# A hybrid decoder layer on one core: six and four feed-forward column tiles by plain products ahead of the seven-product units, in place of four and two

## The chip, the cores and the metric

The kernel runs on one core of a Trainium2 chip. The metric is the device time of one execution in microseconds (us); lower is better. The profile of one further execution is read beside it.

## What is computed

One decoder layer on 512 tokens of width 1024, all in float32. Two SwiGLU feed-forwards with an inner width of 2816 stand around a token mixer (sliding-window attention and a gated causal convolution), and a gated embedding ends the layer. The two feed-forwards are what the change touches:

```python
def swiglu(h, w_gu, w_down):
    g, u = jnp.split(h @ w_gu, 2, axis=-1)
    return (jax.nn.silu(g) * u) @ w_down

def reference(x, p, ffn1_norm, ffn1_wgu, ffn1_wdown, mix_norm, w_in, ...):
    x = x + 0.5 * swiglu(rmsnorm(x, ffn1_norm[i]), ffn1_wgu[i], ffn1_wdown[i])
    ...
    x = x + merged @ w_out[i]
    x = x + 0.5 * swiglu(rmsnorm(x, ffn2_norm[i]), ffn2_wgu[i], ffn2_wdown[i])
    e = rmsnorm(p[i] @ ple_proj[i], ple_norm[i])
    gate = jax.nn.sigmoid(rmsnorm(x, ple_gate_norm[i]) @ ple_gate_w[i])
    x = x + gate * e
```

## The kernel before

Each float32 product is made of three fast ones. Every operand is split into a rounded high part and the remainder (`split_into`: ScalarE writes the high part, VectorE subtracts it to get the low part), and `mm3` adds high times high, low times high and high times low in PSUM. So a weight piece of 128x1024 costs one ScalarE and one VectorE instruction (`whi_wgu`, `wlo_wgu`) before TensorE may use it.

**Two ways to make a feed-forward's gate and up columns.** The 2816 columns are 22 tiles of 128, each with a gate half and an up half.

- A tile by *plain products* (`products`, called from `ffn`): 2 halves x 8 blocks of the width x 3 products = 48 matmuls with 512 tokens moving. It uses the activations before normalization (tiles `h` in the first feed-forward, `f_h` in the second) and multiplies by the norm's factor only when the sums leave PSUM (`gated`: VectorE writes `f_gs` and `f_us`, ScalarE does the SiLU, GpSimd multiplies by the factor). It therefore needs no factor before it starts. Each tile holds two PSUM banks (`f_g`, `f_u`) until `gated` has read them.
- Two tiles by a *unit* (`pair` and `unit`): Strassen's scheme, seven products in place of eight, on halves of the tokens. That is 7 forms x 2 halves x 4 blocks x 3 = 168 matmuls with 256 tokens moving, summed in the banks `wgu_a` and `wgu_b`. It needs sums of weight blocks (two made by accumulating DMAs from GpSimd's queue, two by VectorE in the PSUM tiles `zs_wgu`) and forms of the *normalized* activations: `f_xn` (x times gain times factor), its split `f_nh`, `f_nl`, and the sums and differences `f_t` with their splits `f_t_h`, `f_t_l`. `sums` makes these once for each feed-forward, mostly on VectorE, and they cannot start before the norm's factor is in the PSUM tile `f_n_sp`.

**The order in `ffn`.** Tiles 0 and 1 go by plain products block by block while the norm is computed. Then `plain - 2` further tiles go by plain products, `sums` is recorded, the plain tiles are gated, and the rest goes by units, two tiles at a time. The first down projection of the first four pairs (`down(0, 4)`, tiles `wd`) follows the unit that starts at tile 8, the others the last unit:

```python
PLAIN = 4, 2
DOWNS = {8: [(0, 4)], 20: [(4, 8), (8, 11)]}
```

`PLAIN` gives the number of plain tiles in the first and the second feed-forward; so before there are 9 + 10 = 19 units.

**What sets the order on the engines.** Nothing is run as it is recorded. `record` makes a list of virtual instructions, `plan` and `simulate` order them for each engine by due times worked back from TensorE's order, with numbered slots for buffers (4 for raw weights, 4 each for high and low parts, 8 PSUM banks), and `hybrid_layer` issues them. On the chip each engine then works through its own list in that order. `SUMMED` names the weights of the mixer whose remainder is made by an accumulating DMA (`residue`) and not by VectorE.

Of the kernel before, what the change touches and what calls it, by code (L numbers as in the profile page):

```python
# [20 lines left out]
KD = D // P  # L21
# [379 lines left out]
        op.ls = ls  # L401


SUMMED = dict(wzc=1, wzg=1)
WINDOW = 10
PLAIN = 4, 2
DOWNS = {8: [(0, 4)], 20: [(4, 8), (8, 11)]}
SPARE = 0, 1, 3, 6

# [273 lines left out]
def record():  # L683
    nc = Program()

    def ps_tile(name):
        return nc.tile(name, [P, S], F32, "ps")
# [24 lines left out]
    def split_into(hi, lo, src, scale=None, eng=nc.vector):  # L712
        if scale is None:
            nc.scalar.activation(hi, src, AF.Copy)
            eng.tensor_tensor(lo, src, hi.bitcast(F32), op=ALU.subtract)
        else:
            nc.scalar.activation(hi, src, AF.Copy, scale=scale)
            nc.vector.scalar_tensor_tensor(
                lo, src, scale, hi.bitcast(F32), op0=ALU.mult, op1=ALU.subtract
            )  # L720
# [5 lines left out]

    def piece(key, i, n=PIECE, off=0, cuts=1):

        if key in SUMMED and i % SUMMED[key] == 0:
            return residue(key, i)  # L730
        raw = nc.tile(f"raw_{key}{i}", [P, PIECE], F32, "raw")
        hi = nc.tile(f"whi_{key}{i}", [P, PIECE], F32R, "hi")
        lo = nc.tile(f"wlo_{key}{i}", [P, PIECE], F32R, "lo")
        for c in range(cuts):
            s = slice(c * n // cuts, (c + 1) * n // cuts)
            d = slice(off + s.start, off + s.stop)
            nc.sync.dma_start(raw[:, s], Dram(key)[i][:, d])
            split_into(hi[:, s], lo[:, s], raw[:, s], eng=nc.flex if key in FLEX else nc.vector)
        return hi, lo

    def residue(key, i):

        raw = nc.tile(f"raw_{key}{i}", [P, PIECE], F32, "raw")
        hi = nc.tile(f"whi_{key}{i}", [P, PIECE], F32R, "hi")
        rest = nc.tile(f"wlo_{key}{i}", [P, PIECE], F32R, "lo")
        nc.sync.dma_start(raw, Dram(key)[i])
        nc.scalar.activation(rest, raw, AF.Copy, scale=-1.0)
        nc.scalar.activation(hi, raw, AF.Copy)
        nc.gpsimd.dma_start(rest, raw, accum_op=ALU.add)
        return hi, rest  # L750

    def mm3(ps, w, x, start, stop, first=1, skip=False):

        nc.tensor.matmul(ps, w[first], x[0], start=start, stop=False, skip_group_check=skip)
        nc.tensor.matmul(ps, w[1 - first], x[0], start=False, stop=False, skip_group_check=skip)
        nc.tensor.matmul(ps, w[0], x[1], start=False, stop=stop, skip_group_check=skip)

    def part(w, s):
        return w[0][:, s], w[1][:, s]
# [270 lines left out]
    def ffn(tag, wgu, wdown, h, gain, ss, after, cuts, wide, plain, mid=None):  # L1030
# [9 lines left out]
        def products(i, ks):  # L1040
            if i not in gu:
                gu[i] = ps_tile(f"{tag}_g{i}"), ps_tile(f"{tag}_u{i}")
            for k in ks:
                if k % 4 == 0:
                    ws[i] = piece(wgu, 2 * i + k // 4, cuts=cuts)
                if k == ks[0]:
                    cm = nc.group(f"{tag}_gu{i}_{k}")
                    cm.__enter__()
                c = (k % 4) * 256
                for j, ps in enumerate(gu[i]):  # L1050
                    mm3(
                        ps, part(ws[i], slice(c + j * P, c + (j + 1) * P)), h[k], k == 0, k == KD - 1,
                        0 if cuts > 1 and i == k == 0 else 1,
                    )
            cm.__exit__(None, None, None)
# [93 lines left out]
                first = first or nc.groups[-1].ops[0]  # L1149
        for i in range(plain):  # L1150
            if i > 1:
                products(i, range(4))
                products(i, range(4, KD))
        T, hn = sums(tag, gain, rp)
        for i in range(plain):
            for ps in gu[i]:
# [9 lines left out]
    def next_norm(tag, gain):  # L1166
        h, ss = [None] * KD, SumSq(f"{tag}_ss")

        def after(o):
            h[o] = split(f"{tag}_h{o}", x[o], gain[:, o : o + 1])  # L1170
            ss.in_psum(x[o], KD)

        return h, ss, after

    h2, ss2, after = next_norm("mix", g_mix)
    ffn("f1", "wgu1", "wd1", h, g_ffn1, ss, after, 4, False, PLAIN[0])


    def proj(tag, key, i, h, nk=KD):

        w = piece(key, i)
        ps = ps_tile(tag)
        with nc.group(tag):
            for k in range(nk):
                mm3(ps, part(w, slice(k * P, (k + 1) * P)), h[k], k == 0, k == nk - 1)
        return ps
# [65 lines left out]
    def token_major(tag, key, i0, n_pieces, kper, n):  # L1252

        per = S // n
        banks = [ps_tile(f"{tag}b{b}") for b in range(NT // per)]
        pss = [banks[t % len(banks)][:, (t // len(banks)) * n :][:, 0:n] for t in range(NT)]
        ws = [piece(key, i0 + i) for i in range(n_pieces)]
        with nc.group(tag):
            for t0 in range(0, NT, len(banks)):
                for i in range(n_pieces):  # L1260
                    for kk in range(kper):
                        k = i * kper + kk
                        wk = part(ws[i], slice(kk * n, (kk + 1) * n))
                        for t in range(t0, t0 + len(banks)):
                            xk = part(h2[k], slice(t * P, (t + 1) * P))
                            mm3(pss[t], xk, wk, k == 0, k == KD - 1)
        return pss
# [216 lines left out]
    def embedding(i):  # L1484

        if not pin:
            for k in range(KP):
                t = ftile(f"pin{k}")
                nc.sync.dma_start(t, Dram("pT")[k])
                pin.append(split(f"pin{k}", t))  # L1490
        w = piece("wple", i)
        for j in range(4):
            n = 4 * i + j
            ps = ps_tile(f"e{n}")
            with nc.group(f"e{n}"):
                for k in range(KP):
                    c = (j * KP + k) * P
                    mm3(ps, part(w, slice(c, c + P)), pin[k], k == 0, k == KP - 1)
            e = ftile(f"es{n}")
            nc.scalar.copy(e, ps)  # L1500
            es.append(e)
            sse.add(ps, on_act=True)
        if len(es) == KD:
            rbe = spread("ple", mean_rstd("ple", sse.accs, D))
            for o in range(KD):
                nc.vector.scalar_tensor_tensor(
                    es[o], es[o], g_ple[:, o : o + 1], rbe, op0=ALU.mult, op1=ALU.mult
                )
# [31 lines left out]

    h4, ss4, after4 = next_norm("pg", g_gate)
    ffn("f2", "wgu2", "wd2", h3, g_ffn2, ss3, after4, 1, False, PLAIN[1], lambda: [embedding(i) for i in range(2)])


# [173 lines left out]
```

## Time and profile before

| | |
|---|---|
| median of three runs | 1165.48 us (1165.45 to 1166.0) |
| the profiled execution | 1165.91 us, of which the profile's span is 1164.2 us |
| TensorE matmuls | 7628 records, busy 98% of the span |
| VectorE | busy 84% of the span |
| ScalarE, GpSimd | 62% and 34% |
| granted TensorE clock, mean | 0.995 |

Times within the profile are us from the start of the span. A row of a timeline has the start, the length and the instruction, with output and inputs by the program's names. A row of windows has, for a stretch, the busy time of TensorE (PE), its weight loads (PEld), VectorE (DVE), ScalarE (ACT) and GpSimd (POOL), each with its number of instructions, then the granted TensorE clock (1.00 is full), the busy share of the DMA engines and GB/s. The first feed-forward lies at 5 to 354 us, the mixer up to about 758, the second feed-forward at 758 to about 1110, and the gate of the embedding at the end. Matmuls overlap, so that the time of one is read from the distance between starts and not from its length.

### The profile page before, as it was taken

Reading aid. Unit: us, or ns where it says so; the run is one execution under the profiler, and the core shown is the slowest. Engines: PE = TensorE matmul, PEld = TensorE weight load, DVE = VectorE, ACT = ScalarE, POOL = GpSimd, SP = SyncE. Lnnn points to the kernel's source line nnn. Section 1 sums busy time; section 2 is a strip of 40 time slices with the busy share of each in tenths; the row PEclk is TensorE's granted clock in tenths of the full one; section 3 lists DMA queues with packets and bytes.
Section 4 is the critical chain, followed back from the end, with each engine's and each line's share of the span. In section 5 each row is a group of like instructions: output and inputs, shape, how many; then the busy total and the mean of one; then the engine's idle time right before and its main releaser. Section 6 shows DMA issues by size and latency. Waiting matters only on the chain.

```text
span 1164.2 us, 20217 instructions
## 1 busy us (share of the span) xinstructions
PE 1145.0 (98%) x7628; PEld 1052.0 (90%) x7628; DVE 977.2 (84%) x1660; ACT 722.3 (62%) x1279; POOL 395.0 (34%) x480
## 2 busy tenths in 40 slices
PE   9999999999999999999999999999999999999998
PEld 7889999999998888878888888888999999999976
DVE  7899978889896799988998865589888788679996
ACT  6556446656366699999984753355663566574541
POOL 1523113321113886885687100033221132242000
PEclk9989999999999999999999999999999999999999
DMA  7556666566547472665654532435666665565521
GB/s 242 137 146 163 157 159 152 164 144 177 128 123 190 115 176 64 155 145 127 146 162 121 133 109 91 113 87 137 169 158 162 145 174 127 146 153 142 139 73 73
DMA packets 51363, 163.69 MB, mean 141 GB/s; under 512 B 6208, under 2 KB 10944, under 8 KB 51264
## 3 DMA queue, kind: packets, MB, share of 16 engines
q1 hardware_dynamic: 37584, 114.12, 30.1%
q0 software_dynamic: 13536, 48.24, 24.3%
q8 instruction: 60, 0.98, 0.3%
q14 instruction: 39, 0.32, 0.1%
q10 hardware_dynamic: 144, 0.03, 0.0%
HBM read 143.50 MB, written 2.10 MB: 125 GB/s over the span
## 4 chain that ended last, share of the span: by engine, by line
PE 88%; DVE 7%; ACT 4%; DMA 1%; issue 1%; POOL 0%; DVEq 0%; POOLq 0%; ACTq 0%
PE wgu_b L1605 17%; PE wgu_a L1605 12%; PE wd_b L1605 11%; PE wd_a L1605 8%; PE gb L1605 4%; PE ap L1605 4%; PE cp L1605 4%; PE wo L1605 4%; PE pg L1605 3%; PE cb L1605 3%; PE ga L1605 3%; PE ca L1605 3%; PE q0b L1605 2%; PE q1b L1605 2%; DVE wlo_wgu L1605 2%; PE f_g L1605 2%
## 5 line engine op out<-in xcount | busy, mean ns | idle before, releaser
L1605 DVE TENSOR_TENSOR wlo_wgu<-raw_wgu,whi_wgu 128x1024 fp32r<-128x1024 f32 (+1 forms) x131 | 137.1, 1055 | 38.5 <-ACT whi_wgu L1605 38.5
L1605 ACT ACTIVATE whi_wgu<-raw_wgu 128x1024 fp32r<-128x1024 f32 (+1 forms) x131 | 116.2, 901 | 75.1 <-PE wgu_b L1605 33.3
L1605 PE MATMUL wgu_b<-f_t_h,wlo_wgu 128*128 128x256 f32 x456 | 130.2, 285 | 4.5 <-DVE f_gs L1605 2.2
L1605 PE MATMUL wgu_b<-f_t_l,whi_wgu 128*128 128x256 f32 x456 | 130.0, 285 | 2.2 <-DVE f_t_l L1605 2.2
L1605 POOL DMA_DIRECT2D raw_wgu<-in_wgu x38 | 33.6, 900 | 284.4 <-DVE x L1605 123.2
L1605 PE MATMUL wgu_b<-f_t_h,whi_wgu 128*128 128x256 f32 x456 | 129.5, 284 | 0.0
L1605 ACT ACTIVATE whi_wd<-raw_wd 128x1024 fp32r<-128x1024 f32 (+1 forms) x60 | 59.3, 989 | 94.6 <-PE wd_b L1605 58.5
L1605 POOL TENSOR_TENSOR y<-y,ct 128x511 f32<-128x511 f32 (+27 forms) x90 | 108.2, 1242 | 10.4 <-DVE wlo_wap L1605 3.7
L1605 DVE SCALAR_TENSOR_TENSOR cz<-u,dww,cz 128x510 f32<-128x510 f32 (+28 forms) x145 | 106.6, 735 | 3.3
L1605 PEld LDWEIGHTS wgu_b<-f_t_h,wlo_wgu 128*128 128x128 f32 x456 | 88.0, 193 | 5.4 <-DVE f_gs L1605 1.6
L1605 PEld LDWEIGHTS wgu_b<-f_t_l,whi_wgu 128*128 128x128 f32 x456 | 88.0, 193 | 3.0 <-DVE f_t_l L1605 3.0
L1605 PEld LDWEIGHTS wgu_b<-f_t_h,whi_wgu 128*128 128x128 f32 x456 | 88.1, 193 | 0.0
L1605 PE MATMUL wgu_a<-f_nh,wlo_wgu 128*128 128x256 f32 x304 | 86.1, 283 | 0.0
L1605 PE MATMUL wgu_a<-f_nh,whi_wgu 128*128 128x256 f32 x304 | 86.0, 283 | 0.0
L1605 PE MATMUL wgu_a<-f_nl,whi_wgu 128*128 128x256 f32 x304 | 86.0, 283 | 0.0
L1605 DVE TENSOR_TENSOR wlo_wd<-raw_wd,whi_wd 128x1024 fp32r<-128x1024 f32 (+1 forms) x60 | 69.1, 1151 | 10.0 <-ACT whi_wd L1605 9.6
L1605 PE MATMUL wd_a<-f_f_h,wlo_wd 128*128 128x256 f32 x264 | 74.7, 283 | 0.0
L1605 PE MATMUL wd_a<-f_f_h,whi_wd 128*128 128x256 f32 x264 | 74.7, 283 | 0.0
L1605 PE MATMUL wd_a<-f_f_l,whi_wd 128*128 128x256 f32 x264 | 74.7, 283 | 0.0
L1605 PE MATMUL wd_b<-f_f_h,wlo_wd 128*128 128x256 f32 x264 | 74.7, 283 | 0.0
L1605 PE MATMUL wd_b<-f_f_h,whi_wd 128*128 128x256 f32 x264 | 74.7, 283 | 0.0
L1605 PE MATMUL wd_b<-f_f_l,whi_wd 128*128 128x256 f32 x264 | 74.7, 283 | 0.0
(505 smaller groups left out, 4019.5 us busy)
## 6 DMA issues: line engine op xcount, KB each, us to landing
raw_wgu<-in_wgu SPq DMA_DIRECT2D x80, 512.0 KB, 4.4
raw_wgu<-in_wgu POOLq DMA_DIRECT2D x38, 512.0 KB, 5.5
raw_wd<-in_wd SPq DMA_DIRECT2D x32, 512.0 KB, 4.5
raw_wd<-in_wd POOLq DMA_DIRECT2D x16, 512.0 KB, 5.5
raw_wzc<-in_wzc SPq DMA_DIRECT2D x16, 512.0 KB, 3.7
wlo_wzc<-raw_wzc POOLq DMA_DIRECT2D x16, 512.0 KB, 5.3
raw_wzg<-in_wzg SPq DMA_DIRECT2D x16, 512.0 KB, 4.0
wlo_wzg<-raw_wzg POOLq DMA_DIRECT2D x16, 512.0 KB, 5.2
```

Source lines behind the costliest of these rows:

```text
L1605: made[op] = getattr(engines[op.eng], op.what)(*a, **k)
```

## The change

```diff
-SUMMED = dict(wzc=1, wzg=1)
+SUMMED = dict(wzc=0, wzg=0)
 WINDOW = 10
-PLAIN = 4, 2
+CUT = 4
+PLAIN = 6, 4
...
-        if key in SUMMED and i % SUMMED[key] == 0:
+        if key in SUMMED and i >= SUMMED[key]:
             return residue(key, i)
...
         for i in range(plain):
             if i > 1:
-                products(i, range(4))
-                products(i, range(4, KD))
+                for k in range(0, KD, CUT):
+                    products(i, range(k, k + CUT))
```

The numbers of plain tiles go from 4 and 2 to 6 and 4, so that each feed-forward has one unit less. The condition on `SUMMED` is true for every piece of the two weights in both forms, and with `KD = 8` and `CUT = 4` the loop over `k` gives the same two calls as before.

The engines' lists show it as follows. TensorE's list in the first feed-forward, at the end of the fourth plain tile (`f_u_550`): before, the first unit (`wgu_b`) follows at once.

```order
L1605 MATMUL f_u_550<-h_7_h,wlo_wgu_454 128x512
L1605 MATMUL f_u_550<-h_7_h,whi_wgu_412 128x512
L1605 MATMUL f_u_550<-h_7_l,whi_wgu_412 128x512
L1605 MATMUL wgu_b_648<-f_nh_490,wlo_wgu_1_585 128x256
L1605 MATMUL wgu_b_648<-f_nh_490,whi_wgu_1_473 128x256
L1605 MATMUL wgu_b_648<-f_nl_600,whi_wgu_1_473 128x256
```

In the changed kernel the same place (`f_u_562` is the fourth tile's) goes on to the fifth plain tile, `f_g_673`:

```order
L1606 MATMUL f_u_562<-h_7_h,wlo_wgu_461 128x512
L1606 MATMUL f_u_562<-h_7_h,whi_wgu_414 128x512
L1606 MATMUL f_u_562<-h_7_l,whi_wgu_414 128x512
L1606 MATMUL f_g_673<-h_0_h,wlo_wgu_600 128x512
L1606 MATMUL f_g_673<-h_0_h,whi_wgu_477 128x512
L1606 MATMUL f_g_673<-h_0_l,whi_wgu_477 128x512
```

The first unit comes behind the sixth tile, 96 matmuls later:

```order
L1606 MATMUL f_u_787<-h_7_h,wlo_wgu_705 128x512
L1606 MATMUL f_u_787<-h_7_h,whi_wgu_685 128x512
L1606 MATMUL f_u_787<-h_7_l,whi_wgu_685 128x512
L1606 MATMUL wgu_b_873<-f_nh_504,wlo_wgu_1_744 128x256
L1606 MATMUL wgu_b_873<-f_nh_504,whi_wgu_1_733 128x256
L1606 MATMUL wgu_b_873<-f_nl_756,whi_wgu_1_733 128x256
```

So 96 plain matmuls have moved in ahead of the first unit, and one unit of 168 is gone further on; the second feed-forward does the same. TensorE's list has 7433 rows before and 7289 now, 144 = 2 x (168 - 96) fewer. From the end of the first down projection to the start of the second feed-forward the lists of all engines read as before, but for one ScalarE instruction (the split of the embedding's input, `pin_h`) that stands 18 places later; from the second feed-forward's first down projection on they read as before again.

VectorE's list in the first feed-forward, where it makes the activation forms of the first unit. Before: `zs_wgu` sums weights in PSUM, `f_gs_692` gates the last plain tile, `wlo_wgu_6` and `wlo_wgu_5` are the weights of forms 6 and 5, `f_gs_718` and `f_us_735` belong to the unit's own results.

```order
L1605 SCALAR_TENSOR_TENSOR f_t_0_702<-f_t_0_487,f_xn_529 128x256
L1605 SCALAR_TENSOR_TENSOR f_t_1_715<-f_t_1_505,f_xn_546 128x256
L1605 TENSOR_TENSOR wlo_wgu_6_723<-zs_wgu_0_675,whi_wgu_6_694 128x512
L1605 TENSOR_TENSOR f_gs_718<-wgu_b_648,f_gs_718 128x256
L1605 SCALAR_TENSOR_TENSOR f_t_1_715<-f_t_1_505,f_xn_566 128x256
L1605 TENSOR_TENSOR f_t_0_l<-f_t_0_702,f_t_0_h 128x512
L1605 TENSOR_TENSOR wlo_wgu_6_723<-zs_wgu_1_682,whi_wgu_6_694 128x512
L1605 TENSOR_TENSOR wlo_wgu_5_743<-raw_wgu_21_416,whi_wgu_5_612 128x1024
L1605 TENSOR_TENSOR f_t_1_l<-f_t_1_715,f_t_1_h 128x512
L1605 SCALAR_TENSOR_TENSOR f_us_757<-f_u_550,f_gs_692 128x512
L1605 TENSOR_TENSOR f_t_0_l<-f_t_0_487,f_t_0_h 128x512
L1605 TENSOR_TENSOR f_t_1_l<-f_t_1_505,f_t_1_h 128x512
```

In the changed kernel, `f_gs_875` gates the sixth plain tile, whose bank is `f_g_779`:

```order
L1606 TENSOR_TENSOR wlo_wgu_5_854<-raw_wgu_21_647,whi_wgu_5_828 128x1024
L1606 TENSOR_TENSOR f_t_0_l<-f_t_0_838,f_t_0_h 128x512
L1606 TENSOR_TENSOR f_t_1_l<-f_t_1_845,f_t_1_h 128x512
L1606 TENSOR_TENSOR f_gs_875<-f_g_779,f_n_rb 128x512
L1606 TENSOR_TENSOR f_t_0_l<-f_t_0_494,f_t_0_h 128x512
L1606 TENSOR_TENSOR wlo_wgu_6_892<-zs_wgu_0_820,whi_wgu_6_879 128x512
L1606 TENSOR_TENSOR wlo_wgu_6_892<-zs_wgu_1_830,whi_wgu_6_879 128x512
L1606 TENSOR_TENSOR f_t_1_l<-f_t_1_551,f_t_1_h 128x512
L1606 TENSOR_TENSOR f_gs_917<-wgu_b_873,f_gs_917 128x256
L1606 SCALAR_TENSOR_TENSOR f_us_928<-f_u_787,f_gs_875 128x512
```

The splits of the activation forms (`f_t_0_l`, `f_t_1_l`) and of the weights 5 and 6 stand ahead of the first result of the unit (`f_gs_917`), where before they stood behind it (`f_gs_718`).

VectorE's list in the second feed-forward, from the gating of its plain tiles on. Before (`f_g_8629` and `f_g_8642` are the two plain tiles):

```order
L1605 TENSOR_TENSOR f_gs_8865<-f_g_8629,f_n_rb 128x512
L1605 SCALAR_TENSOR_TENSOR f_t_0_8872<-f_t_0_8737,f_xn_8761 128x256
L1605 SCALAR_TENSOR_TENSOR f_t_0_8872<-f_t_0_8737,f_xn_8772 128x256
L1605 TENSOR_TENSOR f_gs_8883<-f_g_8642,f_n_rb 128x512
L1605 TENSOR_TENSOR wlo_wgu_6_8893<-zs_wgu_0_8662,whi_wgu_6_8848 128x512
L1605 SCALAR_TENSOR_TENSOR f_t_1_8901<-f_t_1_8756,f_xn_8781 128x256
L1605 TENSOR_TENSOR wlo_wgu_6_8893<-zs_wgu_1_8669,whi_wgu_6_8848 128x512
L1605 SCALAR_TENSOR_TENSOR f_t_1_8901<-f_t_1_8756,f_xn_8789 128x256
L1605 TENSOR_TENSOR f_t_0_l<-f_t_0_8872,f_t_0_h 128x512
L1605 TENSOR_TENSOR f_gs_8907<-wgu_b_8859,f_gs_8907 128x256
L1605 SCALAR_TENSOR_TENSOR f_us_8941<-f_u_8636,f_gs_8865 128x512
L1605 TENSOR_TENSOR f_t_1_l<-f_t_1_8901,f_t_1_h 128x512
```

In the changed kernel (`f_g_8880` is the fourth plain tile):

```order
L1606 TENSOR_TENSOR f_t_0_l<-f_t_0_8892,f_t_0_h 128x512
L1606 TENSOR_TENSOR f_t_1_l<-f_t_1_8909,f_t_1_h 128x512
L1606 TENSOR_TENSOR wlo_wgu_6_8948<-zs_wgu_0_8860,whi_wgu_6_8938 128x512
L1606 TENSOR_TENSOR wlo_wgu_6_8948<-zs_wgu_1_8873,whi_wgu_6_8938 128x512
L1606 TENSOR_TENSOR f_t_0_l<-f_t_0_8662,f_t_0_h 128x512
L1606 TENSOR_TENSOR f_t_1_l<-f_t_1_8679,f_t_1_h 128x512
L1606 TENSOR_TENSOR zs_wgu_0_8860<-raw_wgu_12_8803,zs_wgu_0_8860 128x512
L1606 TENSOR_TENSOR f_t_0_l<-f_t_0_8698,f_t_0_h 128x512
L1606 TENSOR_TENSOR f_gs_8975<-f_g_8880,f_n_rb 128x512
L1606 TENSOR_TENSOR zs_wgu_1_8873<-raw_wgu_12_8803,zs_wgu_1_8873 128x512
L1606 TENSOR_TENSOR f_t_1_l<-f_t_1_8717,f_t_1_h 128x512
L1606 TENSOR_TENSOR wlo_wgu_5_9001<-raw_wgu_21_8739,whi_wgu_5_8979 128x1024
```

Here too the splits of the first forms come ahead of the last plain tile's gating (`f_gs_8975`), and no result of the unit stands among them any more.

## The prediction

> **What bounds the kernel now.** I read the page first, for the engine that sets the span.
>
> ```profile
> span 1164.2 us, 20217 instructions
> PE 1145.0 (98%) x7628; PEld 1052.0 (90%) x7628; DVE 977.2 (84%) x1660; ACT 722.3 (62%) x1279; POOL 395.0 (34%) x480
> PEclk9989999999999999999999999999999999999999
> PE 88%; DVE 7%; ACT 4%; DMA 1%; issue 1%; POOL 0%; DVEq 0%; POOLq 0%; ACTq 0%
> ```
>
> TensorE is busy 98% of the span and holds 88% of the chain that ended last; VectorE holds 7% of it. So nearly every added matmul lengthens the kernel, and what can be won is in the few places where TensorE waits for VectorE. The granted clock is below full in one early slice. The windows say where:
>
> ```profile
> core 0: us, PE busy (x) PEld busy (x) DVE busy (x) ACT busy (x) POOL busy (x), PEclk, DMA share, GB/s
> 40.00:80.00 40.00, 36.24 (x232) 33.37 (x231) 38.26 (x59) 24.79 (x43) 19.06 (x21) 0.91 0.45 100
> 240.00:280.00 40.00, 40.00 (x335) 40.00 (x335) 34.04 (x53) 25.15 (x44) 10.45 (x10) 1.00 0.65 159
> 500.00:600.00 100.00, 98.53 (x515) 82.09 (x514) 88.01 (x164) 95.45 (x207) 70.35 (x94) 0.98 0.57 139
> 750.00:800.00 50.00, 47.44 (x265) 40.88 (x265) 42.53 (x74) 27.15 (x46) 14.43 (x16) 1.00 0.42 114
> 800.00:850.00 50.00, 48.72 (x406) 48.52 (x405) 46.41 (x77) 31.03 (x55) 14.05 (x15) 1.00 0.65 151
> ```
>
> In the steady run of units (240 to 280) TensorE never waits, with VectorE at 34.0 of 40 us. At the entry of both feed-forwards (40 to 80, 750 to 850) TensorE loses time; the mixer has a little of it too (500 to 600), with a clock of 0.98. Narrower windows show the first entry, then two of the second:
>
> ```profile
> 56.00:58.00 2.00, 1.14 (x8) 0.77 (x6) 2.00 (x5) 1.13 (x4) 1.49 (x2) 1.00 0.59 61
> 58.00:60.00 2.00, 1.22 (x6) 1.03 (x6) 2.00 (x4) 1.00 (x2) 0.74 (x1) 0.83 0.96 186
> 60.00:62.00 2.00, 0.90 (x5) 0.66 (x4) 2.00 (x4) 1.29 (x3) 0.64 (x1) 0.50 0.37 43
> 62.00:64.00 2.00, 2.00 (x11) 2.00 (x11) 2.00 (x4) 1.05 (x3) 1.31 (x3) 0.50 0.61 234
> 64.00:66.00 2.00, 2.00 (x11) 2.00 (x11) 2.00 (x4) 1.50 (x3) 1.31 (x3) 0.50 0.00 0
> 66.00:68.00 2.00, 2.00 (x18) 2.00 (x17) 1.73 (x3) 0.81 (x1) 1.11 (x1) 0.97 0.63 180
> 784.00:788.00 4.00, 3.05 (x26) 2.85 (x24) 4.00 (x6) 3.99 (x8) 3.01 (x2) 1.00 0.18 36
> 788.00:792.00 4.00, 3.10 (x19) 2.49 (x20) 4.00 (x8) 1.35 (x4) 0.56 (x1) 1.00 0.10 14
> ```
>
> VectorE is busy without a break while TensorE stands: it makes the activation forms of the first unit, and the unit starts before they are there. In the first entry the clock then falls to half, so that even back-to-back matmuls run at 11 in 2 us, where later windows have 18. The waits of the two entries bear this out (the first two rows at 0 to 110 us, the third at 750 to 860 us):
>
> ```profile
> PE wgu_b L1605 <- DVE f_t_l L1605: 1.9, 2, 1.1
> PE wgu_b L1605 <- DVE wlo_wgu L1605: 1.0, 1, 1.0
> PE wgu_b L1605 <- ACT f_gs L1605: 1.3, 1, 1.3
> ```
>
> **The price of the exchange.** The rows below are two starts of the same place in two successive units, one row of three plain products, then the first matmul of the first unit and of the first down projection in each feed-forward.
>
> ```profile
> 236.86 4.32 PE wgu_b L1605 x36
> 257.02 4.32 PE wgu_b L1605 x36
> 30.07 0.68 PE f_g L1605 x3
> 50.76 0.28 PE L1605 MATMUL wgu_b<-f_nh,wlo_wgu 128*128 128x256 f32 x1
> 118.62 0.28 PE L1605 MATMUL wd_b<-f_f,wlo_wd 128*128 128x256 f32 x1
> 781.14 0.28 PE L1605 MATMUL wgu_b<-f_nh,wlo_wgu 128*128 128x256 f32 x1
> 867.52 0.28 PE L1605 MATMUL wd_b<-f_f,wlo_wd 128*128 128x256 f32 x1
> ```
>
> A unit of 168 matmuls takes 257.02 - 236.86 = 20.16 us, 0.120 each. A plain product takes 0.68 / 3 = 0.227 us, so two plain tiles of 48 take 96 x 0.2267 = 21.76 us. Each feed-forward exchanges one unit for two plain tiles: +1.60 us, twice, **+3.2 us**. That is on the path, since TensorE is.
>
> The seven-for-eight saving is small here since 256 columns at 0.120 and 512 at 0.227 leave a fixed 2 x 0.120 - 0.227 = 0.013 us a matmul. The Trainium skill, "TensorE: Matmul & The Clock Gate", section "Back-to-back issue gap", gives a warm gap of N / 2.4 + 2.5 ns, which makes 0.109 and 0.216. By it a unit would take 18.3 us, two tiles 20.7, and the exchange would cost 2.4 each, 4.7 in all, which speaks more against the change than the rows do. The rows differ from it and decide.
>
> **What the entries lose now.** From the first unit to the first down projection lie three units in the first feed-forward (those at tiles 4, 6, 8): 118.62 - 50.76 = 67.86 us against 3 x 20.16 = 60.48, a loss of **7.4 us**. In the second there are four (tiles 2 to 8): 867.52 - 781.14 = 86.38 against 80.64, a loss of **5.7 us**. Together 13.1. Outside these stretches the engines' lists read as before, so 13.1 is all that the change can return.
>
> **Does the added plain work cover them?** Plain tiles need no forms, so the first unit now starts 21.76 us later, while VectorE goes on making forms. What VectorE must do for the added tiles, and for the forms, at the durations of these groups (mean ns behind the busy time; the two rows of `f_gs` and `f_us` give min/median/max):
>
> ```profile
> L1605 DVE TENSOR_TENSOR wlo_wgu<-raw_wgu,whi_wgu 128x1024 fp32r<-128x1024 f32 x99 | 124.8, 1262 | 38.5 <-ACT whi_wgu L1605 38.5
> L1605 DVE TENSOR_TENSOR wlo_wgu<-zs_wgu,whi_wgu 128x512 fp32r<-128x512 f32 x76 | 49.0, 680 | 3.7 <-ACT whi_wgu L1605 3.7
> L1605 DVE TENSOR_TENSOR zs_wgu<-raw_wgu,raw_wgu 128x512 f32<-128x512 f32 x38 | 25.5, 711 | 0.2 <-DMA raw_wgu<-in_wgu 0.2
> L1605 DVE SCALAR_TENSOR_TENSOR f_f_l<-f_us,f_f_h 128x512 fp32r<-128x512 f32 x22 | 19.0, 864 | 0.0
> L1605 DVE TENSOR_TENSOR f_t_l<-f_t,f_t_h 128x512 fp32r<-128x512 f32 x16 | 13.3, 834 | 0.0
> L1605 DVE TENSOR_TENSOR wlo_wgu<-raw_wgu,whi_wgu 128x256 fp32r<-128x256 f32 x32 | 12.3, 418 | 0.0
> L1605 DVE SCALAR_TENSOR_TENSOR f_t<-f_t,f_xn 128x256 f32<-128x256 f32 x16 | 7.5, 504 | 0.0
> L1605 DVE TENSOR_TENSOR f_nl<-f_xn,f_nh 128x512 fp32r<-128x512 f32 x8 | 5.0, 679 | 0.0
> L1605 DVE TENSOR_TENSOR f_gs<-f_g,f_n_rb x4: 678/682/684, 37.4 to 54.7; 128x512 f32<-128x512 f32 x4
> L1605 DVE SCALAR_TENSOR_TENSOR f_us<-f_u,f_gs x4: 678/684/692, 40.5 to 61.2; 128x512 f32<-128x512 f32 x4
> ```
>
> First the balance. A unit costs VectorE 34.04 / 40 x 20.16 = 17.2 us. Two plain tiles cost 16 quarter splits x 0.418 = 6.7 us in the first feed-forward (4 x 1.262 = 5.0 in the second, in whole pieces), four gatings x 0.68 = 2.7, and at most 4 x 0.864 = 3.5 for the activation forms of the down projection, which the 17.2 holds too: 12.9 and 11.2. So VectorE has 4.3 and 6.0 us less to do, and 1.6 more to do it in: 5.9 and 7.6. The second covers its loss of 5.7. The first covers the waits but perhaps not all of 7.4; of that, though, the half clock made at least 1.4 (the 22 matmuls of the windows 62 to 66 took 4.00 / 22 = 0.182 and not 0.120 us each), and that isn't VectorE's work. So the relief is about the size of the loss, with little to spare.
>
> Then the order, laid end to end in the first feed-forward. The fifth tile ends at 50.76 + 10.88 = 61.64, the sixth, and the unit's start, at 72.52. VectorE's list has the gating of the fifth, then three splits `f_nl`, the weights of form 2, `f_us`, two `zs_wgu`, four `f_t`, the weights of form 5, and two `f_t_l`: 0.68 + 3 x 0.68 + 1.26 + 0.68 + 2 x 0.71 + 4 x 0.50 + 1.26 + 2 x 0.83 = 11.0. From 61.9 that ends at 72.9, just when the sixth tile's gating `f_gs_875` can start. Behind it stand two `f_t_l` and two halves of the weights of form 6: 0.68 + 2 x 0.83 + 2 x 0.68 = 3.7, so 76.6. Forms 1 and 2 (48 matmuls, 5.76 us) keep TensorE until 78.28, and form 6 is the next: it is ready 1.7 us ahead, form 5 3 us ahead. Before, TensorE waited for these same splits (the first two waits above).
>
> In the second, the third tile ends at 792.0 and the fourth at 802.9 by the old clock; nothing that form 6 needs stands behind the fourth's gating (the list puts `wlo_wgu_6` and four `f_t_l` ahead of it), and form 5 needs `zs`, one `f_t_l` and `wlo_wgu_5` behind it, 0.68 + 0.71 + 0.83 + 1.26 = 3.5 from 803.2, so 806.7 against 810.1.
>
> The wait of 1.3 there (for ScalarE's `f_gs`) falls in the second unit, and ScalarE was itself late by a load:
>
> ```profile
> 815.33 1.06 ACT L1605 ACTIVATE whi_wgu<-raw_wgu 128x1024 fp32r<-128x1024 f32 x1 [1.53 <-DMA raw_wgu<-in_wgu]
> 34.64 1.41 DVE L1605 SCALAR_TENSOR_TENSOR f_xn<-x,g_all,f_n_sp 128x512 f32<-128x512 f32 x2 [1.13 <-PE f_n_sp L1605]
> ```
>
> That load adds into a buffer which VectorE must have read before. In the changed list VectorE comes to these reads (`zs_wgu`, `wlo_wgu_1` of the second unit) about 10 us behind the 806.7, so near 817, and the second unit starts at 802.9 + 20.2 = 823.1. So this wait goes too.
>
> The queues: two tiles load 4 pieces from SP's queue where a unit loads 4 and adds 2 by GpSimd's, so fewer bytes are moved. In the first feed-forward the four pieces go in 16 parts, and the first unit's loads stand behind them in SP's queue, but are due 21.76 us later too. Other edits (`SUMMED`, `CUT`) change no instruction.
>
> **The sum.** +3.2 - 13.1 = -9.9 with both entries wholly covered. ScalarE, GpSimd and their shared waits will not fit as neatly as VectorE's rows laid end to end. What stays is bounded by nothing and by the whole 13.1; nearest is the steady run, which stays at nothing with VectorE at 85%. I take 0.9. Forecast **-9.0 us**: the profiled execution took 1165.91 (span 1164.2 and 1.7 around it), and would take 1156.9; the median of the runs is 0.43 lower, so **1156.5**.
>
> **The rivals.**
>
> - *The last plain tile's gating holds the queue.* VectorE works in its list's order, so `f_gs_875` stops the splits behind it until the sixth tile ends. For it: the 1.7 us above is the whole margin, and `f_t_l` has a mean of 0.83 where `f_nl` of the same size has 0.68, so these splits can be slowed. Against: 3 us for the next forms. If it costs 2 to 3 us in each entry, the gain is about 5: 1160.5. Chance 0.15.
> - *The clock falls in the new entry too.* The rows show half clock in 58 to 68 with TensorE busy 2.4 of 4 us where it fell (56 to 60), and full clock with 6.2 of 8 in the second entry. A new gap of that kind would cost some 2 us of clock and the gap itself, 1: 1159.5. The Trainium skill (same page, "Part 1: The HAM clock gate") has half rate after an idle window of about 3.4 us; the trace agrees in length, as the clock lost in 58 to 68 is 0.34 + 3 x 1.0 + 0.06 = 3.4 us, or 6.8 us at half rate, two such windows. Chance 0.08.
> - *Slower: the wait moves ahead of the unit.* The fifth tile needs its weights split by VectorE, which from the norm's factor on (34.64, the last row above) has eight `f_xn` and five gatings first. If these came late, TensorE would stand at 50.8 with nothing else to run, and the forms behind would be as late as before. It decides when the waits of both entries together exceed 13.1 - 3.2 = 9.9. With all 13.1 kept, the change costs its 3.2: 1168.7. Against it: 8 x 0.70 + 5 x 0.68 = 9.0 us from 34.6 end at 43.6 and leave 7 us. Chance 0.05.
> - *The change doesn't do what it says.* The lists show 144 fewer matmul rows, so this can hardly be. Below 0.01.
>
> **How the numbers follow.** My forecast (gain 6.5 to 10.5) has 0.72, the others as given. A difference of 0.2%, 2.3 us, is about what a measurement can tell from no change. Faster by more takes the forecast, the clock and most of the first rival: 0.89; within it a remainder of the first and half the third: 0.06; slower 0.05. The range reaches from 1154.0 (all of 9.9, and the clock of 0.98 at 500 to 600, up to 2 us, gone by a shift in time) to 1161.5 (the first rival's end).
>
> **What the changed profile would show.** Two plain tiles more in front of `wgu_b`, whose first matmul stands near 72.5; the first down projection at 112.8 to 114 where it stood at 118.6; no window below 1.9 of 2 us of TensorE in 70 to 90; PEclk at 1.00 there; no `f_t_l` among TensorE's waits; and the second feed-forward's first `wd_b` about 9 us earlier than 867.52. I am wrong if TensorE waits before 72, or if the steady units, whose lists are untouched, are late as well.

## The result and the profile after

The changed kernel took **1156.62 us** (median of four executions, 1154.82 to 1156.88); the kernel before took 1165.74 beside it on the same chip (four, 1165.45 to 1166.08). The ratio is 0.9918, 95% interval 0.9901 to 0.9936: 9.1 us or 0.8% faster. 1156.5 was forecast. The execution profiled is the fastest of the four, 1154.82 us; why it stands 1.8 below the median is the subject of the second experiment.

The page of the changed kernel, its rows for the span, the engines, the granted clock and the chain of what ended last:

```profile
span 1153.1 us, 19900 instructions
PE 1140.8 (99%) x7484; PEld 1043.0 (90%) x7484; DVE 967.0 (84%) x1643; ACT 713.5 (62%) x1267; POOL 398.7 (35%) x481
PEclk9999999999999999999999999999999999999999
PE 94%; ACT 3%; DVE 2%; issue 0%; POOL 0%; DMA 0%; DVEq 0%; POOLq 0%; ACTq 0%
```

There are 144 matmul records fewer, and TensorE has 94% of the chain where it had 88; VectorE's share fell from 7% to 2%. The windows of the same five stretches, then narrow ones of the first entry (columns as before):

```profile
40.00:80.00 40.00, 40.00 (x209) 34.43 (x208) 36.47 (x57) 23.11 (x46) 23.91 (x26) 1.00 0.50 133
240.00:280.00 40.00, 40.00 (x335) 40.00 (x335) 33.98 (x56) 24.47 (x43) 8.32 (x10) 1.00 0.62 157
500.00:600.00 100.00, 98.46 (x521) 82.28 (x522) 89.54 (x155) 94.94 (x203) 70.75 (x93) 1.00 0.58 143
750.00:800.00 50.00, 50.00 (x244) 42.27 (x243) 41.86 (x69) 24.45 (x39) 22.85 (x20) 1.00 0.42 109
800.00:850.00 50.00, 50.00 (x419) 50.00 (x419) 47.05 (x75) 34.07 (x60) 16.29 (x17) 1.00 0.62 161
...
56.00:60.00 4.00, 4.00 (x19) 3.34 (x18) 3.38 (x6) 2.21 (x3) 1.64 (x3) 1.00 1.04 311
...
78.00:80.00 2.00, 2.00 (x19) 2.00 (x19) 2.00 (x3) 2.00 (x5) 2.00 (x2) 1.00 0.01 4
```

TensorE is busy throughout both entries (40.00 of 40 us in the first stretch, 50.00 of 50 in the last two), at full clock. VectorE is still busy nearly all the time there (36.47 of 40): it didn't become idle, it is no longer waited for. The waits of TensorE from 0 to 110 us say the same: beside the wait at the very start for `ones` only one is left, for the weights of the first tiles. From 750 to 860 us there is none.

```profile
PE warm L1606 <- DVE ones L1606: 1.1, 1, 1.1
PE f_g L1606 <- DVE wlo_wgu L1606: 0.3, 1, 0.3
```

The first matmuls of the first unit and of the first down projection in each feed-forward:

```profile
72.29 0.28 PE L1606 MATMUL wgu_b<-f_nh,wlo_wgu 128*128 128x256 f32 x1
112.61 0.28 PE L1606 MATMUL wd_b<-f_f,wlo_wd 128*128 128x256 f32 x1
795.51 0.28 PE L1606 MATMUL wgu_b<-f_nh,wlo_wgu 128*128 128x256 f32 x1
855.99 0.28 PE L1606 MATMUL wd_b<-f_f,wlo_wd 128*128 128x256 f32 x1
```

From these and the rows of before the whole difference between the two traces can be laid out:

| stretch | before | after | difference |
|---|---|---|---|
| start to the fifth tile's place | 50.76 | 72.29 - 21.76 = 50.53 | -0.2 |
| from there to the first down projection | 67.86 | 62.08 | -7.4 of loss, +1.6 of exchange |
| to the place of the second feed-forward's third tile | 662.52 | 795.51 - 21.76 - 112.61 = 661.14 | -1.4 |
| from there to its first down projection | 86.38 | 82.24 | -5.7 of loss, +1.6 of exchange |
| to the end of the span | 296.7 | 297.1 | +0.4 |
| sum | 1164.2 | 1153.1 | -11.1 |

Two units in the first feed-forward took 112.61 - 72.29 = 40.32 us and three in the second 60.48, which is 2 and 3 times 20.16 to the last digit: **both entry losses are wholly gone**. The exchange and the losses make -9.9. The -1.4 in the mixer is in the main the clock's: the row 500 to 600 has 0.98 before and 1.00 here, by a stretch of 3.41 us at half clock, which is 1.7 us of work. Most executions of the changed kernel have such a stretch as well, as the second experiment shows.

### The profile page after: what moved, and what is told of

Its sections match the earlier page's. It is cut to its first block, busy times and chain, and to the rows that moved or that the text cites. A ratio compares the mean times of both kernels' runs of the same rounds, so it can differ in the third digit from the quotient of the medians.

```text
span 1153.1 us, 19900 instructions
## 1 busy us (share of the span) xinstructions
PE 1140.8 (99%) x7484; PEld 1043.0 (90%) x7484; DVE 967.0 (84%) x1643; ACT 713.5 (62%) x1267; POOL 398.7 (35%) x481
## 4 chain that ended last, share of the span: by engine, by line
PE 94%; ACT 3%; DVE 2%; issue 0%; POOL 0%; DMA 0%; DVEq 0%; POOLq 0%; ACTq 0%
PE wgu_b L1606 17%; PE wgu_a L1606 12%; PE wd_b L1606 10%; PE wd_a L1606 8%; PE f_g L1606 5%; PE f_u L1606 5%; PE gb L1606 4%; PE ap L1606 4%; PE wo L1606 4%; PE cp L1606 4%; PE pg L1606 3%; PE cb L1606 3%; PE ga L1606 3%; PE ca L1606 3%; PE q0b L1606 2%; PE q1b L1606 2%
## 5 line engine op out<-in xcount | busy, mean ns | idle before, releaser
L1606 PE MATMUL wgu_b<-f_t_h,wlo_wgu 128*128 128x256 f32 x408 | 115.5, 283 | 0.0
L1606 PE MATMUL wgu_b<-f_t_l,whi_wgu 128*128 128x256 f32 x408 | 115.5, 283 | 0.0
L1606 PE MATMUL wgu_b<-f_t_h,whi_wgu 128*128 128x256 f32 x408 | 115.5, 283 | 0.0
L1606 POOL DMA_DIRECT2D raw_wgu<-in_wgu x34 | 29.8, 876 | 175.2 <-DMA raw_wgu<-in_wgu 53.3
L1606 PEld LDWEIGHTS wgu_b<-f_t_h,whi_wgu 128*128 128x128 f32 x408 | 78.3, 192 | 0.0
L1606 PEld LDWEIGHTS wgu_b<-f_t_h,wlo_wgu 128*128 128x128 f32 x408 | 78.3, 192 | 0.0
L1606 PEld LDWEIGHTS wgu_b<-f_t_l,whi_wgu 128*128 128x128 f32 x408 | 78.3, 192 | 0.0
L1606 PE MATMUL wgu_a<-f_nl,whi_wgu 128*128 128x256 f32 x272 | 77.0, 283 | 0.0
L1606 PE MATMUL wgu_a<-f_nh,wlo_wgu 128*128 128x256 f32 x272 | 77.0, 283 | 0.0
L1606 PE MATMUL wgu_a<-f_nh,whi_wgu 128*128 128x256 f32 x272 | 77.0, 283 | 0.0
```

Source lines behind the costliest of these rows:

```text
L1606: made[op] = getattr(engines[op.eng], op.what)(*a, **k)
```

## The experiments

Each ran beside the kernel before on the same chip, so "gain" is against the before of its own session (1165.94 to 1166.18). The ratios have 95% intervals.

| kernel | median, us | ratio |
|---|---|---|
| 6 and 2 plain tiles (two sessions) | 1161.93, 1160.46 | 0.9962 (0.9949 to 0.9975), 0.9957 (0.9942 to 0.9972) |
| 4 and 4 plain tiles | 1162.62 | 0.9973 (0.9963 to 0.9983) |
| two plain tiles behind two units | 1169.73 | 1.0038 (1.0025 to 1.0052) |
| 8 and 6 plain tiles | 1158.05 | 0.9937 (0.9925 to 0.9950) |
| the changed kernel again | 1156.59 | 0.9923 (0.9911 to 0.9936) |
| with 10 idle VectorE instructions | 1157.53 | 0.9930 (0.9915 to 0.9945) |
| with 26 | 1162.63 | 0.9982 (0.9973 to 0.9991) |
| 4 and 2, three remainders by DMA | 1160.08 | 0.9957 (0.9944 to 0.9969) |
| 6 and 2, the embedding ahead | 1160.44 | 0.9949 (0.9935 to 0.9962) |

### Is it the place or the number of the plain tiles?

The same matmuls as the changed kernel's, but the two further plain tiles of each feed-forward stand behind the first two units:

```diff
-PLAIN = 6, 4
+PLAIN = 4, 2
+LATE_AT = 4
...
-            pair(i, T, hn)
+            if i == plain + LATE_AT:
+                for j in (i, i + 1):
+                    for k in range(0, KD, CUT):
+                        products(j, range(k, k + CUT))
+                    for ps in gu[j]:
+                        ps.vt.late = True
+                    gated(j)
+            else:
+                pair(i, T, hn)
```

> As many plain tiles and as few units as in the changed kernel, so the same matmuls and the same work of VectorE in all, but two of the plain tiles of each feed-forward stand behind the first two units, not ahead of the first. Theory (position is what counts: cover at the entry): both entries lose as before, and the exchange costs its 3.2: 1165.7 + 3.2 = 1168.9 us. Rival (amount is what counts: fewer units, less work for VectorE and GpSimd, fewer bytes): the gain stays, about 1156.6. A part of it, some 1162 to 1166, would say that the second unit's forms, which the plain tiles here do cover, held a share of the loss.

It took 1169.73 us, 3.7 **slower** than before. The four landmarks of its trace:

```profile
50.95 0.28 PE L1615 MATMUL wgu_b<-f_nh,wlo_wgu 128*128 128x256 f32 x1
121.33 0.28 PE L1615 MATMUL wd_b<-f_f,wlo_wd 128*128 128x256 f32 x1
782.51 0.28 PE L1615 MATMUL wgu_b<-f_nh,wlo_wgu 128*128 128x256 f32 x1
871.07 0.28 PE L1615 MATMUL wd_b<-f_f,wlo_wd 128*128 128x256 f32 x1
```

The first stretch holds two units and two plain tiles, 62.08 us of work, and took 70.38; the second three units and two tiles, 82.24, and took 88.56. So 8.3 and 6.3 us are lost, a little more than before (7.4 and 5.7), and the exchange is paid on top. The number of plain tiles and units is that of the changed kernel: it is their place ahead of the first unit that brings the gain.

### Each feed-forward alone, and the clock

```diff
-PLAIN = 6, 4
+PLAIN = 6, 2
```

> Only the first feed-forward is changed (6 and 2 plain tiles in place of 4 and 2). Theory (plain tiles ahead of the first unit cover VectorE's making of the forms; each exchange costs 1.6 us of TensorE, the returned entry loss is 7.4): 1165.7 - 7.4 + 1.6 = 1159.9 us, with the first feed-forward's first wd_b at about 112.8 and the second's entry (780 to 870) still losing 5.7 us of matmul time. Rival A (a shift of time only moves the half clock, and most of the gain is the clock's): 1163 or more, since the waits were 4 us or less. Rival B (the gain is VectorE's lighter load in the second feed-forward): no gain here, 1167.3.

```diff
-PLAIN = 6, 4
+PLAIN = 4, 4
```

> Only the second feed-forward is changed (4 and 4 plain tiles in place of 4 and 2). Theory (cover): 1165.7 - 5.7 + 1.6 = 1161.6 us, first entry unchanged with its half clock between 58 and 68 us, first wd_b of the second feed-forward at 4.1 us below 867.5. If the two exchanges are independent, the gains of this kernel and of the one with the first feed-forward alone add up to the 9.1 of both. Rival (they help each other, or the 9.1 comes from one of them): a gain of 0 or of more than 7 here.

In five executions the first feed-forward alone gained 4.1 us (5.8 expected), the second alone in nine 3.4 (4.1 expected). Neither rival holds, but together they give 7.4 where both changes together give 9.1 to 9.4. The second one's trace has what was expected, a gap of exactly three units and the down projection 4.2 us ahead of 867.52:

```profile
802.88 0.28 PE L1606 MATMUL wgu_b<-f_nh,wlo_wgu 128*128 128x256 f32 x1
863.35 0.28 PE L1606 MATMUL wd_b<-f_f,wlo_wd 128*128 128x256 f32 x1
```

The gain by its median is 0.8 us less than that. About 0.4 of this lies outside the profile's span: its executions take 2.0 to 2.1 us more than their spans, those of the kernel before 1.7. The rest stays open. The first one's trace also has what was expected: 113.12 - 72.81 = 40.31 us for two units, and 860.48 - 774.30 = 86.18 in the second entry, a loss of 5.5. But its five executions fell apart by their mean clock: 1159.18 at 0.999 and 1159.71 at 0.997, three at 1161.9 to 1162.5 at 0.996, and the one with a trace was the first. So it was run again for a trace of one of these:

> Only the first feed-forward changed, a second time, for a trace of an execution at a mean clock near 0.996 (three of its five had that, and 1162; the one traced had 0.999 and 1159.2). Open is why the two exchanges done alone bring 4.1 and 3.4 and together 9.1 to 9.4. Theory (the waits that stay in the second entry now let the clock fall there, where they didn't before): half clock behind the wait at 501 and again in 780 to 795, 3.4 us of time each, and a time near 1162. Rival (something else of 2 us): no half clock in 780 to 795 in an execution of 1162.

The median of these three executions was 1160.46, a gain of 5.7, so that with these executions the two gains add up to 9.1. The traced one took 1163.04 us at 0.995. Three of its windows, then the second feed-forward's landmarks:

```profile
504.00:508.00 4.00, 4.00 (x28) 3.33 (x25) 4.00 (x11) 3.97 (x8) 3.67 (x4) 0.59 0.71 137
784.00:788.00 4.00, 3.48 (x17) 3.31 (x16) 4.00 (x8) 1.42 (x3) 1.32 (x2) 0.58 0.71 239
815.00:819.00 4.00, 4.00 (x23) 4.00 (x23) 3.35 (x6) 0.89 (x2) 1.28 (x2) 0.57 0.18 74
...
775.67 0.28 PE L1606 MATMUL wgu_b<-f_nh,wlo_wgu 128*128 128x256 f32 x1
864.31 0.28 PE L1606 MATMUL wd_b<-f_f,wlo_wd 128*128 128x256 f32 x1
```

The clock falls three times: behind the mixer's wait near 501, and twice in the second entry, whose waits this kernel still has (the fall near 815 was not in the expectation). There the same four units lose 88.64 - 80.64 = 8.0 us. They lost 5.7 in the trace of before and 5.5 in the other trace of this same kernel, in both of which the clock stayed full. So waits that are left cost more in some executions than in others. That accounts for the missing 1.7 to 1.9 us of the first session in kind; how often it happens was not counted with traces.

The same question for the changed kernel itself, whose executions differ by 2 us:

> The changed kernel once more, to see what its own executions differ by. Theory (the spread of 2 us is one window of half clock of 3.4 us behind the wait of 1.8 us near 501, which some executions have and some don't): times in two groups, near 1154.9 at a mean clock of 0.999 and near 1156.6 at 0.997 to 0.998, 1.7 apart. Rival (the spread is in the entries or in the loads): times spread evenly, and no relation to the mean clock.

1155.08 us at a clock of 0.999 and four executions of 1156.5 to 1157.4 at 0.997 to 0.998; with the first session it is two of nine at 1154.8 and 1155.1 and seven at 1156.5 or more. The trace is of one at 1156.59. The window with the mixer's wait near 501 (TensorE busy 2.45 of 4 us) and the one behind it, and below them the same two of the trace of 1154.82:

```profile
500.00:504.00 4.00, 2.45 (x34) 2.17 (x35) 2.52 (x5) 4.00 (x9) 3.71 (x4) 1.00 0.62 207
504.00:508.00 4.00, 4.00 (x26) 3.35 (x24) 4.00 (x12) 3.97 (x8) 3.67 (x4) 0.57 0.72 139
```

```profile
500.00:504.00 4.00, 2.46 (x35) 2.16 (x37) 2.52 (x6) 4.00 (x9) 3.71 (x4) 1.00 0.60 204
504.00:508.00 4.00, 4.00 (x30) 3.37 (x27) 4.00 (x11) 3.97 (x8) 3.67 (x4) 1.00 0.68 129
```

The same wait ahead, the same engines busy, and behind it four matmuls fewer at 0.57. The two spans, 1154.9 and 1153.1, differ by 1.8: the 3.41 us of half clock (at half rate, 1.7 us of work) and 0.1. By the landmarks 1.6 of the difference arises between the first down projection (112.61 and 112.78) and the second feed-forward's first unit (795.51 and 797.26). The 1.8 by which the profiled execution lay under the median is this.

The kernel before has two levels as well: of its 38 executions in the three later sessions 12 took 1163.8 to 1164.7 us at 0.998, and 26 took 1165.7 to 1166.8 at 0.994 to 0.996; the trace of before is of one at 0.995. So the gain can be read level by level: 9.2 us between the lower ones (medians 1164.2 and 1154.95) and 9.4 between the upper ones (1166.2 and 1156.8).

### What is the exchange worth by itself?

```diff
-PLAIN = 6, 4
+PLAIN = 8, 6
```

> Two more plain tiles ahead in each feed-forward (8 and 6). Theory: after the change neither entry loses anything that a trace shows, so two further exchanges cost their full 2 x 1.6 = 3.2 us: 1156.7 + 3.2 = 1159.9 us. Rival (there is still a hidden loss that more cover returns, or the exchange costs less than the row says): 1156.7 or less. Rival (the exchange costs more, as the page's shorter gaps would have it, 4.7 for two): 1161.4.

1158.05 us, 1.4 more than the changed kernel's median, and not 3.2. But its five executions all have a clock of 0.999 or 1.0, where seven of the changed kernel's nine have lost, by their mean clock, what the window above costs (one of the seven has a trace). Against the changed kernel's two at 0.999 (1154.82 and 1155.08) it is 3.0 to 3.2 slower, the price of two exchanges. The rivals (a hidden loss that more cover returns, 4.7 for two) fall. The landmarks show why nothing was left to win, two units in 40.31 us:

```profile
819.72 0.28 PE L1606 MATMUL wgu_b<-f_nh,wlo_wgu 128*128 128x256 f32 x1
860.03 0.28 PE L1606 MATMUL wd_b<-f_f,wlo_wd 128*128 128x256 f32 x1
```

### How much room is there?

The prediction laid VectorE's rows end to end and came to a margin of 1.7 us. VectorE's rows of the changed kernel around it, from the sixth tile's gating on:

```profile
71.81 0.69 DVE L1606 TENSOR_TENSOR f_gs<-f_g,f_n_rb 128x512 f32<-128x512 f32 x1
72.42 0.68 DVE L1606 TENSOR_TENSOR f_t_l<-f_t,f_t_h 128x512 fp32r<-128x512 f32 x1
73.18 1.29 DVE L1606 TENSOR_TENSOR wlo_wgu<-zs_wgu,whi_wgu 128x512 fp32r<-128x512 f32 x2
74.39 1.69 DVE L1606 TENSOR_TENSOR f_t_l<-f_t,f_t_h 128x512 fp32r<-128x512 f32 x1
76.00 0.41 DVE L1606 TENSOR_TENSOR f_gs<-wgu_b,f_gs 128x256 f32<-128x256 f32 x1
...
79.99 0.41 DVE L1606 TENSOR_TENSOR f_us<-wgu_b,f_us 128x256 f32<-128x256 f32 x1
```

Two kernels delay the instructions behind the first of these rows by idle work on a tile of its own (10 and 26 instructions):

```diff
             made[op] = getattr(engines[op.eng], op.what)(*a, **k)
+            if op is gate:
+                for _ in range(STALL):
+                    nc.vector.tensor_tensor(idle, idle, idle, op=ALU.mult)
```

> The changed kernel with 10 small VectorE instructions on a buffer of their own, about 2 us in all, right behind the sixth plain tile's f_gs in the first feed-forward. In the changed kernel's trace the splits behind it end 2.9 us (the second f_t_l, 76.08 against 79.0) and 2.5 us (the weights of form 3, 82.79 against 85.25) before TensorE needs them. Theory (this margin covers): no change, 1156.6, and no wait of TensorE in 70 to 90 us. Rival (the engines have no slack there, VectorE sets the pace): +2 us, 1158.6.

> The same with 26 instructions, about 5 us. Theory: the delay less the margin of 2.5, so 2.5 us of waits at forms 6 and 3 of the first unit, 1159.1, more if the clock falls on the gap (up to 1.7 a window). By the replay in the prediction, with a margin of 1.7: 3.3 us. Rival (the cover is much larger than that, the plain tiles bring more than they need to): no change, 1156.6.

They took 1157.53 and 1162.63 us, by medians 0.9 and 6.0 more than the changed kernel beside them. The 0.9 is within the spread of the clock: two of the four executions with 10 are at 0.999 (1156.78 and 1156.83), and against the changed kernel's two at 0.999 they cost 1.7 to 2.0. So both expectations, nothing and 2.5, fail. The size of the first rival, 2, is met, by another sum than its own; the second's, nothing, is not. The traces say why. With 10 (three of VectorE's rows, then TensorE's waits from 60 to 110 us):

```profile
72.45 3.23 DVE L1613 TENSOR_TENSOR idle<-idle 128x128 f32<-128x128 f32 x10
78.21 0.41 DVE L1610 TENSOR_TENSOR f_gs<-wgu_b,f_gs 128x256 f32<-128x256 f32 x1
82.19 0.41 DVE L1610 TENSOR_TENSOR f_us<-wgu_b,f_us 128x256 f32<-128x256 f32 x1
...
PE wgu_b L1610 <- DVE f_us L1610: 0.9, 1, 0.9
PE wgu_b L1610 <- DVE f_gs L1610: 0.4, 1, 0.4
```

With 26 (the delay, the first read, the wait, and one window):

```profile
73.01 8.45 DVE L1613 TENSOR_TENSOR idle<-idle 128x128 f32<-128x128 f32 x26
83.95 0.41 DVE L1610 TENSOR_TENSOR f_gs<-wgu_b,f_gs 128x256 f32<-128x256 f32 x1
...
PE wgu_b L1610 <- DVE f_gs L1610: 5.6, 1, 5.6
...
84.00:88.00 4.00, 3.58 (x17) 3.59 (x18) 4.00 (x7) 2.28 (x5) 2.96 (x3) 0.50 0.01 2
```

First, the delays were 0.32 us an instruction, 3.2 and 8.4 in all, and not the 0.2 that I had taken. Second, what TensorE waits for is neither a split nor a weight but `f_gs<-wgu_b` and `f_us<-wgu_b`: VectorE must read the unit's first results, of the gate and of the up half, out of their banks before form 6 may add to them, and these reads stand behind the splits in VectorE's list. In the changed kernel the first read ends at 76.00 + 0.41 = 76.41, and form 6 starts at 72.29 + 48 x 0.12 = 78.05: 1.6 us of margin. The second ends at 79.99 + 0.41 = 80.40, and form 6's up half starts at 72.29 + 72 x 0.12 = 80.93: **0.5 us of margin**, the smaller of the two. In the second entry the same two reads end at 799.42 and 803.24, which leaves 1.9 and 0.9.

With 10 both reads end 2.2 us later (78.62 and 82.60). The other 1.0 us of the delay is made up on the way, mostly since the `f_t_l` ahead of the first read takes 0.89 us there and not 1.69. A shift of 2.2 is past the first margin by about 0.5 (0.4 measured) and past the second by 1.7; TensorE loses 0.4 and 0.9 in the two waits, and 1.8 from the first unit to the first down projection (114.43 - 72.32 = 42.11 us for two units). With 26 the first read ends at 84.36, in a trace in which VectorE's row ahead of the delay stands 0.6 later (the delay starts at 73.01 and not 72.42): 84.36 - 78.65 = 5.7 expected of such a rule, 5.6 measured. From 10 to 26 the delay grows by 5.2 us and the first wait by 5.2, so past the margin it goes through one to one. And the large gap draws the clock down (0.50 in 84 to 88), as the first entry of before did: this trace loses 120.97 - 72.88 - 40.32 = 7.8 us between the same landmarks, some 2 more than the wait.

### Could VectorE be relieved without the exchange?

Four and two plain tiles as before, but for forms 1, 2 and 5 of each feed-forward's first unit the low part of the weights is made by an accumulating DMA:

```diff
+                if early and f in RESTS:
+                    hi, rest = done[f]
+                    nc.scalar.activation(rest, raw, AF.Copy, scale=-1.0)
+                    nc.scalar.activation(hi, raw, AF.Copy)
+                    nc.gpsimd.dma_start(rest, raw, accum_op=ALU.add)
+                else:
+                    split_into(*done[f], raw)
```

> Not the change but another way to lighten VectorE at the entries: 4 and 2 plain tiles as before, and the low parts of the weights of forms 1, 2 and 5 of the first unit of each feed-forward made by an accumulating DMA (ScalarE writes the negated high part, the DMA adds the raw weights), as the mixer does it. VectorE has 3 x 1.26 = 3.8 us less to do in each entry, ScalarE 3 x 1.06 more, and no exchange is paid. Theory (the entry's loss is VectorE's work that came too late): losses of 7.4 and 5.7 fall by 3.8 each, 1165.7 - 7.6 = 1158.1, or up to 2 less if the clock doesn't fall. Rival A (only the plain tiles' position can cover, since the chain of norm factor, forms and splits is what is late and not the load on VectorE): as before, 1165.7. Rival B (the DMA lands later than VectorE would have been done): slower than before, new waits of the unit for these loads.

1160.08 us, a gain of 5.9 where 7.6 was expected. Rival A falls, and so does B's outcome, a slower kernel. Its waits, the first two from 0 to 110 us, the third from 750 to 860, and a row of ScalarE in the first entry:

```profile
PE wgu_b L1614 <- DVE f_gs L1614: 1.8, 1, 1.8
PE wgu_b L1614 <- ACT f_gs L1614: 1.1, 1, 1.1
...
PE wgu_b L1614 <- DVE wlo_wgu L1614: 1.7, 1, 1.7
...
62.91 1.06 ACT L1614 ACTIVATE whi_wgu<-raw_wgu 128x1024 fp32r<-128x1024 f32 x1 [3.98 <-DMA raw_wgu<-in_wgu]
```

Less work on VectorE alone also pays, so the loss was VectorE's lateness and nothing particular to plain tiles. The traced execution is the slowest of the five (1162.04). In it the second entry loses 863.62 - 779.97 - 80.64 = 3.0 us (5.7 before) and the first 5.8 (7.4 before; 51.26 to 118.99 for three units and 1.4 us of the down projection, which here moved ahead of the last unit's end), with the clock full in both. The largest wait left is again the read of the unit's first result, behind the splits. The wait for ScalarE's `f_gs` is new in the first entry: the last row stands just ahead of this `f_gs`, and ScalarE had been idle for 3.98 us until a load landed, so something of rival B's kind takes a part of the gain. That the added DMAs delay this load was not shown.

### A version made from the explanation

Six plain tiles in the first feed-forward, two in the second, and there the embedding's 48 matmuls, which need no norm, ahead of the first unit (its norm, `embedding_norm`, stays where it was):

```diff
-PLAIN = 6, 4
+PLAIN = 6, 2
...
+        if early:
+            early()
         T, hn = sums(tag, gain, rp)
...
-    ffn("f2", ..., lambda: [embedding(i) for i in range(2)])
+    ffn("f2", ..., embedding_norm, lambda: [embedding(i) for i in range(2)])
```

> A version made from the explanation: 6 plain tiles in the first feed-forward as in the change, but only 2 in the second, and there the 48 matmuls of the embedding (10.9 us of TensorE that need no norm factor, recorded near the end of the second feed-forward before) stand ahead of the first unit in place of two more plain tiles. Theory (any work of TensorE that waits for nothing covers the entry; 10.9 us against a loss of 5.7): the second entry's loss is gone without its exchange of 1.6, so 1156.6 - 1.6 = 1155.0, or some 1 less if the waits where the embedding stood before (1.6 us at 1000 to 1020) go as well. Rival (10.9 us of cover is too little, or the embedding's own splits and copies on VectorE and ScalarE use it up): a loss of 2 to 5 us at the second entry, 1157 to 1160.

1160.44 us: 3.8 slower than the changed kernel, and the same as 6 and 2 plain tiles without the embedding ahead (1160.46 in the same session). The second entry (two landmarks) and a new wait in the mixer, from 560 to 700 us:

```profile
789.98 0.28 PE L1609 MATMUL wgu_b<-f_nh,wlo_wgu 128*128 128x256 f32 x1
873.95 0.28 PE L1609 MATMUL wd_b<-f_f,wlo_wd 128*128 128x256 f32 x1
...
PE ap L1609 <- DVE wlo_wap L1609: 2.3, 1, 2.3
```

The entry still loses 83.97 - 80.64 = 3.3 us (2.4 less than before): 10.9 us of cover were too little here, as the rival had it. And what the entry gained is lost elsewhere: weights of the mixer (`wlo_wap`) are 2.3 us late, where neither the kernel before nor the changed one waits. The likely cause is that the plan of the whole program came out otherwise; it was not followed further.

## Why the prediction was right

- **The exchange, +1.6 twice.** Right. Units take 20.16 us in the changed kernel too (40.32 / 2), two further exchanges cost 3.0 to 3.2 at equal clock, and the same tiles without the cover made the kernel 3.7 slower. The Trainium skill, "TensorE: Matmul & The Clock Gate", section "Back-to-back issue gap", calls the formula that the prediction set beside these rows the gap of an isolated matmul. So the 4.7 worked out from it was no price for a stream of matmuls, and the runs don't show it.
- **The entries lose 13.1, and the plain tiles cover it.** Right in mechanism: the same tiles in another place bring nothing, and less work for VectorE without them brings a part. The balance of VectorE, which left it open whether the first loss would be covered in full, was pessimistic: both are at nothing.
- **0.9 taken as staying.** This is the one term that was mis-sized: 0.0 stays. That the median still came out at the forecast is partly luck: by the sum without it the gain would have been 9.9, and it was 9.1. The two traces that both have the mixer's half clock differ by 1164.2 - 1154.9 = 9.3 for 9.9; the 0.6 between lies outside the entries (the end alone differs by 0.4 in the table above) and was not followed further.
- **The replay of VectorE's list.** It said that the last splits end at 76.6 with 1.7 us to spare; they end at 76.08, 2.0 us ahead of form 6. But the replay left out what stands next in the list, the reads of the unit's first results, and these have only 1.6 and 0.5 us. So the size was about right for the first read, three times too large for the second, and the consumer was wrong. The waits of before had this read already, in rows that the prediction doesn't list (the first from 0 to 110 us, the second, the largest there, from 750 to 860):

```profile
PE wgu_b L1605 <- DVE f_gs L1605: 0.8, 1, 0.8
PE wgu_b L1605 <- DVE f_gs L1605: 1.4, 1, 1.4
```

- **The landmarks.** First unit near 72.5: 72.29. First down projection at 112.8 to 114: 112.61, 0.2 below the range, since nothing stayed and the unit itself started 0.2 earlier. The second's about 9 us ahead of 867.52: 11.5, of which 1.4 is the mixer's clock. Nothing of `f_t_l` among the waits, no window below 1.9 of 2 us, PEclk 1.00: all so. The wait for ScalarE's `f_gs` in the second unit went too.
- **The rivals.** The gating that holds the queue: not met, though 0.5 us of margin is all that kept it off in the first entry, as the delays show. The clock in the new entry: not met, but real, since a gap of 5.6 us there draws it down. The wait ahead of the unit: not met, TensorE is busy without a break from 40 on. The loss of clock in the mixer, which the range's low end held as perhaps gone, is gone in two of nine executions.

## What to carry to other kernels

A loss at the entry to a steady run is the lateness of the engine that prepares for it: measure it between two landmarks of the bound engine, as the excess over a multiple of the steady period. Work that needs no preparation covers it at the price of that work's lower efficiency, but only ahead of the first wait and only if there is enough of it; two units later it paid the price here and covered nothing. When an in-order list is replayed, include the reads that free a PSUM bank and not only the writes that feed the next matmul. And where executions differ by their mean clock, compare those of equal clock before reading a difference of 1 us.

## What the runs showed of the hardware

- The granted clock falls for whole windows of 3.41 us: in the clock records of all these traces the stretches at half clock within the run last 3.41 or 6.83 us, and the full ones between them are whole multiples too (498.35 = 146 windows, 645.12 = 189, 443.73 = 130). The same program with the same wait (1.5 to 1.6 us near 501) lost such a window in one execution and not in another; why the one and not the other no run here shows. A wait of 1.5 us so costs 1.5 or 3.2 us, which is a spread of two levels and not noise.
- So it was too in the second entry of the kernel with 6 and 2 plain tiles: in one trace TensorE was busy 2.10 of 4 us (780 to 784) and the clock stayed at 1.00, in the other 2.62 of 4, and the next 4 us had 0.58. A stretch's clock in one trace is no promise for the next.
- Short dependent VectorE instructions of 128x128 took 0.32 us from start to start, half of the 0.61 from a 128x512 one to the next in the rows above (71.81 to 72.42).
